# A two-layer streaming trunk on one core: the second chunk's loads queued behind the first's at the turn to the down products, and low parts and norm sums moved from POOL to DVE

## The chip, the cores and the metric

One core of a Trainium2 chip runs the whole program. The metric is the device time of one execution in microseconds (us). The engines are PE (TensorE: matmuls, with weight loads in PEld), DVE (VectorE), ACT (ScalarE), POOL (GpSimd) and SP (SyncE, which issues all the DMAs here). Each engine works through its own instructions in the order in which the program was written out; between engines, semaphores decide.

## The reference

Two layers on 1088 tokens (1024 of a prompt, 64 of running streams) with 1024 channels, in 32-bit floats. Layer 0 mixes tokens with a diagonal state-space model (S5) that ends in a gated linear unit, layer 1 with attention that has forget gates (FoX). Each is followed by a ConvFFN with 2816 hidden channels. Cut to what matters:

```python
def s5_mixer(...):            # layer 0
    ...
    val, gate = jnp.split(g @ w_glu, 2, axis=-1)
    return val * jax.nn.sigmoid(gate), ...

def fox_prompt(...):          # layer 1
    ...
    return o @ w_o, k, v, logf

def conv_ffn(x, hist, w_up, w_gate, conv_w, conv_b, w_down):
    a = x @ w_up
    ... # conv: three taps along the tokens
    h = jax.nn.gelu(conv + conv_b) * (x @ w_gate)
    return h @ w_down, a_pad[:, -(CONV_WIDTH - 1):]

for i in range(DEPTH):
    xp = xp + mixer(rms_norm(xp, norm_mix[i]))
    xp = xp + conv_ffn(rms_norm(xp, norm_ffn[i]), ...)
y = rms_norm(xp, norm_final)  # the same for xs, the 64 tokens of running streams
```

## The kernel before

**Numbers.** A 32-bit product is made of three matmuls on rounded parts: each operand is split into a high part (ACT copies it to a rounded type) and a low part (operand minus high part). hi x hi, hi x lo and lo x hi are added up in a PSUM bank. The 1088 tokens lie in four chunks of 272 columns, the channels on the 128 partitions. `k.x[d]` is the residual of channel block d, of 8.

**Plain weights.** `unit` (L116) loads a block of weights of 128 x 1024 (L121), makes hi on ACT (L125) and lo on POOL (L126). `kunit` calls it for the gated linear unit (GLU), for the query, key and value projections (qkv) and for the output projection (`wo`); `plain_unit` calls it for three pairs of hidden channel blocks of the down product. There are 85 such subtracts: 32 in GLU, 25 in qkv, 16 in wo, 6 in each FFN. The pools of raw, hi and lo have 2, 3 and 3 buffers.

**Seven products.** The other FFN weights go through Strassen's scheme: a product of 2 x 2 blocks is made of 7 block products instead of 8 (`SUMS`, j in the order 0, 1, 3, 2, 5, 4, 6). `left_factors` makes the 7 left factors of a weight block: POOL forms four sums (L312 to L315), ACT the high parts (L303) and DVE the low parts (L304). Its buffers of hi and lo are those of `unit`. `to_forms` makes the right factors of the normed input (L232, L233 the split, L239 the norm's scaling, L258 to L264 the sums), and `store_forms` those of a hidden pair (L473, L474, L481 to L487).

**The FFN.** A loop over the 11 hidden pairs fp makes up and gate products on PE (L335 in `block`); `channels` collects them, L554 multiplies the two, and `store_forms` writes the 7 forms of the pair to DRAM (544 KB each). The down products take the pairs in four chunks, `PCH` = (0, 1), (10, 2), (3, 4), (5, 6); pairs 7 to 9 are done plainly. `load(ci)` (L430) issues the loads of a chunk's forms: those of chunk 0 and 2 go to `k.R`, the buffers of the normed input's forms, which come free as the last gate products have read them; in the rows they are xh and xl. Those of chunk 1 and 3 go to `k.E` (e) or to a buffer b. The last pair, 10, stays in SBUF, so chunk 1 loads 7 forms only. `load(0)` is called in the last pass of the loop, and `load(ci + 1)` at the head of the down loop's pass ci. `reload` (L425) brings back residual blocks that were put aside in DRAM. The adds of down products into the residual are L585, on DVE; they free PE's PSUM banks. I call the place where PE goes from the last gate products to the down products the turn; the transpose of the conv tail (L564) stands between the two.

**Norm sums.** `Norm.add` squares a new residual block on ACT (L167) and adds it to a running sum (L168), on POOL for odd d and on DVE for even d. The GLU calls it after L1210 and L1212, the output projection after L1568.

**Order.** The order of instructions on each engine isn't the one of the text. A scheduler walks through the program with a model of the engines' times and writes out a fixed order for each engine; it may exchange instructions that do not depend on each other. All DMAs here are issued by SP, in eight lanes taken in turn: an issue waits until the transfer eight places before it has landed.

Of the kernel before, what the change touches and what calls it, by code (L numbers as in the profile page):

```python
# [9 lines left out]

F32 = mybir.dt.float32
F32R = mybir.dt.float32r
# [103 lines left out]
def unit(k, src, a, b, raw=None, to=None):  # L116

    nc = k.nc
    if raw is None:
        raw = k.wraw.tile([P, KT, 2 * P], F32, name="raw").rearrange("p a b -> p (a b)")[:, :a * b].rearrange("p (a b) -> p a b", b=b)  # L120
        nc.sync.dma_start(raw, src)  # L121
    if to is None:
        to = [q.tile([P, KT, P], F32R, name=m).rearrange("p a b -> p (a b)") for q, m in ((k.whi, "hi"), (k.wlo, "lo"))]
    hi, lo = (t[:, :a * b].rearrange("p (a b) -> p a b", b=b) for t in to)
    nc.scalar.activation(hi, raw, AF.Copy)  # L125
    nc.gpsimd.tensor_tensor(lo, raw, hi.bitcast(F32), op=OP.subtract)  # L126
    return hi, lo


# [274 lines left out]
def ffn(k, layer, norm, after, prepare=lambda: None):  # L404
# [11 lines left out]
    with ExitStack() as ctx:  # L416
# [10 lines left out]
                k.x[d] = xtile(k, d)[:, :T]  # L427
                nc.sync.dma_start(k.x[d], k.xD[d])

        def load(ci):  # L430

            for m, (j, _) in enumerate(SUMS):
                for n, fp in enumerate(PCH[ci]):
                    if (fp, j) in slots:
                        continue
                    if ci % 2 == 0:
                        t = k.R[2 + 2 * m + n]
                    elif 7 * n + m < 12:
                        t = k.E[7 * n + m]
                    else:  # L440
                        t = k.big.tile([P, T], F32R, name="b")
                    slots[fp, j] = t
                    nc.sync.dma_start(t.bitcast(F32), fD[fp][j])

        def load_plain(fps, tiles):
            for fp in fps:
# [100 lines left out]
        for fp in range(FP):  # L547
            cs, gs = channels(fp, None if fp else k.entry)
            if fp == FP - 1:
                unit0 = down_unit(0, 0)  # L550
                load(0)
            for c, g in zip(cs, gs):
                for o, w, s in parts(0, T):
                    v.tensor_tensor(g[:, o:o + w], c[:, o + 2 * s:o + 2 * s + w], g[:, o:o + w], op=OP.mult)  # L554
            turn = itertools.cycle((lambda: xtile(k, 2), lambda: xtile(k, 3), lambda: k.big.tile([P, T], F32, name="b")))
            if fp == FP - 1:
                reload((2, 3))
                store_forms(fp, gs)
            else:
                (store_plain if fp in PLAIN else store_forms)(fp, gs, lambda: next(turn)())  # L560
# [42 lines left out]

        for ci, fps in enumerate(PCH):
            if ci + 1 < len(PCH):
                load(ci + 1)
            else:
                load_plain(PLAIN[:1], iter(k.R[2:6]))
            for u in range(2):
                w = down_unit(ci, u) if ci or u else unit0  # L610
                for dd in range(2):
                    down(w, 2 * u + dd, dd * P, fps, (0, 1))
# [554 lines left out]
def glu(k, norm, after):  # L1167
# [13 lines left out]
    with tc.tile_pool(name="gl", bufs=1) as pool:  # L1181
        for a, hs in enumerate(HALVES):
            for d in range(KT):
                if d % 2 == 0:
                    raws = load((d * P, D + d * P), 1 if a or d else 2)
                wv, wg = (unit(k, None, KT, P, r[:, :, d % 2 * P:d % 2 * P + P]) for r in raws)
                if a == 0 and d == 4:
                    k.cw = [conv_params(k, pool, k.bank(), i) for i in range(2)]
                ps = {}

                def products(n, kts):
                    if n not in ps:
                        ps[n] = [k.bank() for i in range(2)]
                    for p, u in zip(ps[n], (wv, wg)):
                        dense(k, p, u, *NCH[n], kts)
                if a == 0 and d == 0:
                    for kts in (range(KT - 1), (KT - 1,)):
                        for n in hs:
                            products(n, kts)
                for n in hs:  # L1200
                    o, m = NCH[n]
                    if n not in ps:
                        products(n, range(KT))
                    if a == 0 and n == 0:
                        for i in (0, 1) if d == 0 else (d + 1,) if d + 1 < KT else ():
                            k.nc.sync.dma_start(k.x[i], k.x0D[i])
                    pv, pg = ps[n]
                    s = k.tmp.tile([P, CW], F32, name="tm")[:, :m]
                    nc.scalar.activation(s, pg[:, :m], AF.Sigmoid)
                    nc.vector.tensor_tensor(s, s, pv[:, :m], op=OP.mult)  # L1210
                    x = k.x[d][:, o:o + m]
                    nc.vector.tensor_tensor(x, x, s, op=OP.add)  # L1212
                    norm.add(n, d)
                if a and d < 2:
                    next(k.entry, None)
            k.entry = after(a)
# [341 lines left out]
def wo(k, norm, after):  # L1558
    nc, tc = k.nc, k.tc
    for a, hs in enumerate(HALVES):  # L1560
        for d in range(KT):
            u = kunit(k, k.I["fox_w_o"][0], d * P)
            for n in hs:
# [2 lines left out]
                dense(k, ps, u, o, m)  # L1566
                x = k.x[d][:, o:o + m]
                nc.vector.tensor_tensor(x, x, ps[:, :m], op=OP.add)  # L1568
                norm.add(n, d)
            if a and d < 2:  # L1570
                next(k.entry, None)
        k.entry = after(a)
# [119 lines left out]
```

## Time and profile before

| | us |
|---|---|
| median of 3 runs | 2690.65 |
| lowest, highest | 2681.59, 2690.93 |
| profiled execution | 2694.2 |
| its span | 2692.4 |

The stages of the span, roughly, in us:

| stage | from | to |
|---|---|---|
| state-space mixer | 0 | 290 |
| GLU | 290 | 505 |
| FFN 0, up and gate products | 497 | 977 |
| FFN 0, down products in four chunks | 977 | 1175 |
| FFN 0, plain down products | 1175 | 1240 |
| qkv (25 units) | 1240 | 1550 |
| attention | 1550 | 1835 |
| output projection | 1835 | 1937 |
| FFN 1, up and gate products | 1937 | 2421 |
| FFN 1, down products and final norm | 2421 | 2692 |

The profile shows one execution. An engine's busy share is an average over all stages; what a change in one stage is worth is read from that stage's rows. A number in brackets behind an instruction in the timeline is the time that its engine had waited for nothing else, and what released it. PEclk is the clock that TensorE was granted, as a share of full speed, 2.4 GHz.

### The profile page before, as it was taken

How to read it: one execution, taken by the hardware profiler on the slowest of the kernel's cores; microseconds unless marked ns; L12 is line 12 of the kernel's file. 1: busy time of each engine (PE TensorE's matmuls, PEld its weight loads, DVE VectorE, ACT ScalarE, POOL GpSimd, SP SyncE). 2: the span in 40 equal slices, each digit the busy share in tenths (PEclk: the TensorE clock that was granted, in tenths of full speed). 3: DMA queues.
4: the chain of work that ended last, by engine and by line, in shares of the span. 5: the costliest groups of instructions: out<-in, count | busy, mean ns of one | idle time of the engine just before them, and what ended most of it. 6: DMA issues, size and time to landing. Idle time of an engine off the chain costs nothing. (4 is left out here: it accounts for less than half of the span.)

```text
span 2692.4 us, 52353 instructions
## 1 busy us (share of the span) xinstructions
PE 2570.8 (95%) x20646; PEld 2418.3 (90%) x20646; DVE 1813.3 (67%) x3534; ACT 1127.4 (42%) x2190; POOL 1045.2 (39%) x938
## 2 busy tenths in 40 slices
PE   7788899999999999999999999999999999999998
PEld 4676899899999999999999966668999999999998
DVE  5899426878877668755322178883788877668865
ACT  5444324454444431124222277773454545441213
POOL 4576445533222222235212167774542222222222
PEclk9878999999999999999999999999999999999999
DMA  5112523234433377335686667753314433347531
GB/s 146 46 38 59 163 78 114 63 119 166 154 116 139 106 272 260 100 107 162 180 225 183 179 166 196 192 145 122 112 64 147 179 131 139 114 168 292 197 114 67
DMA packets 265739, 385.28 MB, mean 143 GB/s; under 512 B 27980, under 2 KB 210244, under 8 KB 265492
## 3 DMA queue, kind: packets, MB, share of 16 engines
q1 hardware_dynamic: 265492, 381.92, 45.1%
q8 instruction: 163, 2.67, 0.4%
q14 instruction: 84, 0.69, 0.1%
HBM read 251.31 MB, written 121.50 MB: 138 GB/s over the span
## 5 line engine op out<-in xcount | busy, mean ns | idle before, releaser
L335 PE MATMUL mm<-e,hi 128*128 128x272 f32 x2464 | 476.4, 290 | 7.2 <-ACT hi L303 7.2
L136 PE MATMUL mm<-xh,hi 128*128 128x272 f32 x1408 | 407.0, 290 | 1.6 <-DVE tm L1500 1.0
L138 PE MATMUL mm<-xh,lo 128*128 128x272 f32 x1408 | 404.7, 289 | 1.5 <-POOL lo L126 1.5
L335 PEld LDWEIGHTS mm<-e,hi 128*128 128x128 f32 x2464 | 387.6, 189 | 7.9 <-ACT hi L303 7.8
L137 PE MATMUL mm<-xl,hi 128*128 128x272 f32 x1280 | 368.8, 289 | 0.0
L335 PE MATMUL mm<-e,lo 128*128 128x272 f32 x1232 | 353.6, 289 | 2.4 <-DVE lo L304 2.4
L335 PE MATMUL mm<-xh,hi 128*128 128x272 f32 x1792 | 351.1, 291 | 2.7 <-DVE x L509 2.7
L303 ACT ACTIVATE hi<-raw 128x1024 fp32r<-128x1024 f32 x186 | 196.1, 1056 | 316.0 <-PE mm L335 254.3
L126 POOL TENSOR_TENSOR lo<-raw,hi 128x1024 fp32r<-128x1024 f32 (+1 forms) x83 | 198.6, 2398 | 327.9 <-ACT hi L125 303.7
L314 POOL TENSOR_TENSOR raw<-s,raw 128x512 f32<-128x512 f32 x62 | 91.0, 1468 | 581.3 <-DVE lo L304 580.0
L335 PE MATMUL mm<-xl,hi 128*128 128x272 f32 x1440 | 283.2, 291 | 15.5 <-DMA xl<-fD 9.5
L335 PEld LDWEIGHTS mm<-xh,hi 128*128 128x128 f32 x1792 | 284.5, 190 | 4.0 <-DVE x L509 3.5
L136 PEld LDWEIGHTS mm<-xh,hi 128*128 128x128 f32 x1408 | 265.6, 189 | 2.9 <-DVE tm L1500 1.5
L138 PEld LDWEIGHTS mm<-xh,lo 128*128 128x128 f32 x1408 | 264.7, 189 | 2.1 <-POOL lo L126 2.1
L304 DVE TENSOR_TENSOR lo<-raw,hi 128x1024 fp32r<-128x1024 f32 x186 | 245.3, 1319 | 22.9 <-ACT hi L303 22.8
L335 PE MATMUL mm<-xh,lo 128*128 128x272 f32 x896 | 258.8, 291 | 1.0 <-DVE lo L304 1.0
L585 DVE TENSOR_TENSOR x<-x,mm 128x272 f32<-128x272 f32 x512 | 201.9, 433 | 65.9 <-PE mm L335 63.9
L335 PEld LDWEIGHTS mm<-xl,hi 128*128 128x128 f32 x1440 | 229.0, 191 | 17.2 <-ACT e L473 9.9
L137 PEld LDWEIGHTS mm<-xl,hi 128*128 128x128 f32 x1280 | 241.6, 189 | 0.1
L335 PEld LDWEIGHTS mm<-e,lo 128*128 128x128 f32 x1232 | 232.2, 189 | 2.6 <-DVE lo L304 2.6
L335 PE MATMUL mm<-xl,lo 128*128 128x272 f32 x720 | 209.6, 292 | 0.0
L312 POOL TENSOR_TENSOR s<-raw 128x512 f32<-128x512 f32 x62 | 82.5, 1331 | 292.6 <-DVE s1l L304 274.6
(423 smaller groups left out, 6096.3 us busy)
## 6 DMA issues: line engine op xcount, KB each, us to landing
fD<-x SPq DMA_DIRECT2D x82, 544.0 KB
e<-fD SPq DMA_DIRECT2D x50, 544.0 KB
raw<-in_ffn_w_up SPq DMA_DIRECT2D x24, 1024.0 KB
raw<-in_ffn_w_gate SPq DMA_DIRECT2D x22, 1024.0 KB
fD<-b SPq DMA_DIRECT2D x40, 544.0 KB
xh<-fD SPq DMA_DIRECT2D x32, 544.0 KB
xl<-fD SPq DMA_DIRECT2D x32, 544.0 KB
raw<-in_ffn_w_down SPq DMA_DIRECT2D x64, 256.0 KB
```

Of the source, the lines that this page charges most:

```text
L126: nc.gpsimd.tensor_tensor(lo, raw, hi.bitcast(F32), op=OP.subtract)
L136: mm(ps, h, rh, start=first, stop=False)
L137: mm(ps, h, rl, start=False, stop=False)
L138: mm(ps, l, rh, start=False, stop=last)
L303: nc.scalar.activation(h, t, AF.Copy)
L304: nc.vector.tensor_tensor(l, t, h.bitcast(F32), op=OP.subtract)
L312: add(s1, a21, a22, op=OP.add)
L314: add(a11, s1, a11, op=OP.subtract)
L335: k.nc.tensor.matmul(bank[:, :CW], x, y, start=j not in (2, 4, 6) and n == 0 and i == 0, stop=n == last and i == 2, skip_group_check=True)
L585: v.tensor_tensor(x, x, bank[:, :m], op=OP.add)
```

## The change

Three edits:

- `load` links each load to the one before it with an order-only edge (`issue_after`): the scheduler has to keep the loads of a chunk in the order of the text and those of the next chunk behind them. `queued` carries the last load on to the next chunk.
- In `unit`, the low part (L126) is made by DVE instead of POOL.
- The norm sums of GLU and output projection (L168) are on DVE for every d; those of the other stages stay as they were.

```diff
@@ unit @@
     nc.scalar.activation(hi, raw, AF.Copy)
-    nc.gpsimd.tensor_tensor(lo, raw, hi.bitcast(F32), op=OP.subtract)
+    nc.vector.tensor_tensor(lo, raw, hi.bitcast(F32), op=OP.subtract)
     return hi, lo
@@ load @@
-        def load(ci):
+        def load(ci, ins=None):
...
                     slots[fp, j] = t
-                    nc.sync.dma_start(t.bitcast(F32), fD[fp][j])
+                    with tc.issue_after(ins) if ins else nullcontext():
+                        ins = nc.sync.dma_start(t.bitcast(F32), fD[fp][j]).ins
+            return ins
@@ ffn @@
                 unit0 = down_unit(0, 0)
-                load(0)
+                queued = load(0)
...
             if ci + 1 < len(PCH):
-                load(ci + 1)
+                queued = load(ci + 1, queued)
@@ glu @@
-                    norm.add(n, d)
+                    norm.add(n, d, k.nc.vector)
@@ wo @@
-                norm.add(n, d)
+                norm.add(n, d, nc.vector)
```

POOL's instructions go from 940 to 823 and DVE's from 3536 to 3653; PE's and SP's stay the same in number. The lines of the changed kernel are two higher behind `load`.

SP at the turn of layer 0, before: fD is the DRAM copy of the forms, and its second number the pair; xl_2018 and xl_2306 are the buffers of slot 4 of the seven sums, xl_2595 and xl_2820 of slot 5, xl_2946 and xl_2985 of slot 6.

```order
190 L443 DMA e_3057<-fD_2_5300 128x1088
191 L443 DMA xl_1730<-fD_1_5299 128x1088
192 L443 DMA xl_1442<-fD_0_5298 128x1088
193 L443 DMA e_3059<-fD_2_5300 128x1088
194 L443 DMA e_3058<-fD_2_5300 128x1088
195 L443 DMA b<-fD_2_5300 128x1088
196 L443 DMA xl_2306<-fD_1_5299 128x1088
197 L443 DMA xl_2018<-fD_0_5298 128x1088
198 L443 DMA e_3061<-fD_2_5300 128x1088
199 L443 DMA e_3060<-fD_2_5300 128x1088
200 L443 DMA xl_2820<-fD_1_5299 128x1088
201 L443 DMA xl_2595<-fD_0_5298 128x1088
```

The same place after:

```order
190 L444 DMA xl_1442<-fD_0_5298 128x1088
191 L444 DMA xl_1730<-fD_1_5299 128x1088
192 L444 DMA xl_2018<-fD_0_5298 128x1088
193 L444 DMA xl_2306<-fD_1_5299 128x1088
194 L444 DMA xl_2595<-fD_0_5298 128x1088
195 L444 DMA xl_2820<-fD_1_5299 128x1088
196 L428 DMA x_10797<-xD 128x1088
197 L444 DMA xl_2946<-fD_0_5298 128x1088
198 L444 DMA xl_2985<-fD_1_5299 128x1088
199 L444 DMA e_3057<-fD_2_5300 128x1088
```

All loads of pair 2 (e and b) have moved behind those of pairs 0 and 1, the pair of each slot has changed places, and a residual reload (x_10797) stands ahead of slot 6. The turn of layer 1 has the same pattern.

DVE at the same turn, before: L474 makes the low parts of the last pair's forms, L481 to L487 their sums, L585 adds down products to the residual.

```order
934 L474 TENSOR_TENSOR e_3051<-b,e_3051 128x544
935 L585 TENSOR_TENSOR x_3033<-x_3033,mm 128x272
936 L474 TENSOR_TENSOR e_3054<-b,e_3054 128x544
937 L481 TENSOR_TENSOR b<-b 128x544
938 L483 TENSOR_TENSOR b<-b 128x544
939 L474 TENSOR_TENSOR e_3052<-b,e_3052 128x544
940 L484 TENSOR_TENSOR b<-b 128x544
941 L474 TENSOR_TENSOR e_3055<-b,e_3055 128x544
942 L487 TENSOR_TENSOR b<-b 128x544
943 L474 TENSOR_TENSOR e_3053<-b,e_3053 128x544
944 L474 TENSOR_TENSOR e_3056<-b,e_3056 128x544
945 L585 TENSOR_TENSOR x_10552<-x_10552,mm 128x272 x2
```

After (L476 is the old L474, L483 and so on L481, L587 L585):

```order
975 L476 TENSOR_TENSOR e_3054<-b,e_3054 128x544
976 L587 TENSOR_TENSOR x_10554<-x_10554,mm 128x272 x2
977 L483 TENSOR_TENSOR b<-b 128x544
978 L587 TENSOR_TENSOR x_10552<-x_10552,mm 128x272 x2
979 L485 TENSOR_TENSOR b<-b 128x544
980 L587 TENSOR_TENSOR x_3034<-x_3034,mm 128x272
981 L476 TENSOR_TENSOR e_3052<-b,e_3052 128x544
982 L587 TENSOR_TENSOR x_3034<-x_3034,mm 128x272
983 L486 TENSOR_TENSOR b<-b 128x544
984 L587 TENSOR_TENSOR x_10552<-x_10552,mm 128x272
985 L587 TENSOR_TENSOR x_3033<-x_3033,mm 128x272
986 L587 TENSOR_TENSOR x_10552<-x_10552,mm 128x272
```

The adds that stood behind all pieces of the last pair now stand between them.

POOL at the end of the output projection, before: L312 to L315 are the sums of the first up weight's left factors in FFN 1.

```order
695 L126 TENSOR_TENSOR lo<-raw,hi 128x1024
696 L168 TENSOR_TENSOR s<-s,tm 128x272
697 L126 TENSOR_TENSOR lo<-raw,hi 128x1024
698 L233 TENSOR_TENSOR e_21682<-b,e_21681 128x544
699 L312 TENSOR_TENSOR s<-raw 128x512
700 L168 TENSOR_TENSOR s<-s,tm 128x272
701 L313 TENSOR_TENSOR raw<-raw 128x4x128
702 L168 TENSOR_TENSOR s<-s,tm 128x272
703 L314 TENSOR_TENSOR raw<-s,raw 128x4x128
704 L315 TENSOR_TENSOR raw<-raw 128x4x128
```

After:

```order
599 L233 TENSOR_TENSOR e_21676<-b,e_21675 128x544 x2
600 L233 TENSOR_TENSOR e_21682<-b,e_21681 128x544
601 L312 TENSOR_TENSOR s<-raw 128x512
602 L313 TENSOR_TENSOR raw<-raw 128x4x128
603 L233 TENSOR_TENSOR e_21682<-b,e_21681 128x544
604 L314 TENSOR_TENSOR raw<-s,raw 128x4x128
605 L315 TENSOR_TENSOR raw<-raw 128x4x128
```

The subtracts (L126) and norm sums (L168) are gone from POOL, and nothing but one split stands between its four weight sums. They stand on DVE, among the splits and sums of `to_forms`.

## Rows read from the trace of the kernel before

**Rows 1.** The page's part 1: busy time, share of the span and instructions.

```profile
PE 2570.8 (95%) x20646; PEld 2418.3 (90%) x20646; DVE 1813.3 (67%) x3534; ACT 1127.4 (42%) x2190; POOL 1045.2 (39%) x938
```

**Rows 2.** What PE waited for, 960 to 2693 us: total, times, longest.

```profile
PE mm L335 <- DMA xl<-fD: 9.5, 2, 5.1
```

**Rows 3.** Timeline of PE at both turns: start, length, instruction, wait before it.

```profile
981.60 0.40 PE L335 MATMUL mm<-xh,lo 128*128 128x272 f32 x1 [0.98 <-DVE lo L304]
...
988.81 0.79 PE L335 MATMUL mm<-xl,hi 128*128 128x272 f32 x2 [4.45 <-DMA xl<-fD]
...
2432.82 0.79 PE L335 MATMUL mm<-xl,hi 128*128 128x272 f32 x2 [5.08 <-DMA xl<-fD]
```

**Rows 4.** Timeline of SP's DMA issues at the turn of layer 0.

```profile
973.15 1.02 SPq L443 DMA_DIRECT2D e<-fD  x2
975.15 0.32 SPq L443 DMA_DIRECT2D b<-fD  x1
976.55 1.68 SPq L443 DMA_DIRECT2D xl<-fD  x2
979.26 1.68 SPq L443 DMA_DIRECT2D e<-fD  x2
```

**Rows 5.** Stretches of both turns: busy by engine, then clock, DMA share, GB/s.

```profile
core 0: us, PE busy (x) PEld busy (x) DVE busy (x) ACT busy (x) POOL busy (x), PEclk, DMA share, GB/s
976.00:988.00 12.00, 7.38 (x57) 6.93 (x56) 11.93 (x21) 3.69 (x7) 1.51 (x1) 1.00 1.03 411
988.00:996.00 8.00, 7.19 (x36) 7.22 (x37) 5.87 (x11) 1.91 (x3) 0.00 (x0) 0.57 0.92 357
996.00:1010.00 14.00, 14.00 (x115) 14.00 (x114) 11.06 (x24) 3.82 (x4) 5.21 (x4) 1.00 0.56 191
...
2420.00:2432.00 12.00, 7.74 (x61) 7.33 (x59) 11.93 (x22) 4.29 (x7) 0.00 (x0) 0.99 1.03 408
2432.00:2440.00 8.00, 7.18 (x36) 7.21 (x37) 5.34 (x10) 1.32 (x2) 0.00 (x0) 0.58 1.03 408
2440.00:2454.00 14.00, 14.00 (x114) 14.00 (x113) 11.65 (x24) 3.70 (x4) 4.31 (x4) 1.00 0.58 202
```

**Rows 6.** Groups by line and shape: count, busy us, mean ns, idle before.

```profile
L126 POOL TENSOR_TENSOR lo<-raw,hi 128x1024 fp32r<-128x1024 f32 x80 | 193.5, 2423 | 313.7 <-ACT hi L125 289.5 <-DMA raw<-in_ssm_w_glu 17.1 <-PE y L1126 5.6
L168 POOL TENSOR_TENSOR s<-s,tm 128x272 f32<-128x272 f32 x62 | 52.9, 853 | 90.1 <-ACT tm L167 88.4 <-DMA raw<-in_ssm_w_glu 1.7
L304 DVE TENSOR_TENSOR lo<-raw,hi 128x1024 fp32r<-128x1024 f32 x186 | 245.3, 1319 | 22.9 <-ACT hi L303 22.8
L585 DVE TENSOR_TENSOR x<-x,mm 128x272 f32<-128x272 f32 x512 | 201.9, 433 | 65.9 <-PE mm L335 63.9
L1313 DVE TENSOR_TENSOR ql<-pe,qh 128x272 fp32r<-128x272 f32 x32 | 22.7, 730 | 48.3 <-DMA kD<-ql 31.3 <-ACT qh L1312 17.0
```

**Rows 7.** Who waited for L126 (us, times), over the whole span.

```profile
PE mm L138: 1.5, 2
```

**Rows 8.** Stretches at the end of the output projection, columns as in rows 5.

```profile
1896.00:1928.00 32.00, 32.00 (x255) 31.77 (x254) 31.39 (x45) 14.59 (x25) 20.21 (x12) 1.00 0.46 151
1928.00:1940.00 12.00, 8.62 (x69) 8.40 (x68) 8.47 (x10) 4.87 (x9) 10.21 (x7) 1.00 0.01 2
1940.00:1948.00 8.00, 6.75 (x34) 6.72 (x34) 4.83 (x11) 3.35 (x7) 4.80 (x4) 0.57 0.42 132
```

**Rows 9.** There: timelines of POOL, DVE and PE, and the chain of waits between.

```profile
1920.53 2.74 POOL L126 TENSOR_TENSOR lo<-raw,hi 128x1024 fp32r<-128x1024 f32 x1 [2.36 <-ACT hi L125]
...
1921.28 2.58 DVE L264 TENSOR_TENSOR b<-b 128x544 f32<-128x544 f32 x1
...
1928.07 0.77 POOL s L168
...
1930.10 1.13 POOL s L168
1931.23 0.54 issue
...
1941.25 0.82 PE L335 MATMUL mm<-e,hi 128*128 128x272 f32 x2 [4.63 <-ACT hi L303]
```

More of the change, by code (lines that the diff above doesn't have):

```diff
@@ L8 @@
 import math
-from contextlib import ExitStack, contextmanager
+from contextlib import ExitStack, contextmanager, nullcontext
 F32 = mybir.dt.float32
```

## The prediction

> **What bounds the kernel now.** I read the engine totals first. PE is busy for 2570.8 of 2692.4 us, DVE for 1813.3 and POOL for 1045.2 [rows 1], so a change pays only where PE waits, or where a wait drops PE's clock afterwards. The second view is the list of what PE waited for behind the first gate products: the largest entry is the loads of stored forms, 9.5 us in two waits [rows 2]. The timeline of PE has both, at the turn from the gate products to the down products of each layer: 4.45 us before 988.81 and 5.08 us before 2432.82 [rows 3]. Ahead of the first stands a wait of 0.98 us for a low part from DVE. The third view, stretches of each turn, tells what else is lost: behind the wait the granted clock is 0.57 and 0.58 of full speed for 8 us, which is mostly the lower level, 1.2 GHz, and 1.00 in the stretch after it, 2.4 GHz [rows 5]. PE does 36 matmuls in 7.19 us there and 115 in 14.00 us later; at the later rate the 36 would take 36 x 14.00 / 115 = 4.4 us, so the clock costs 2.8 us a turn. The DMA share is 1.03 with some 410 GB/s through the wait, so the load is late because the transfers run back to back and the needed one stands far back among them.
>
> The same reading at the end of the output projection gives a second place: PE waits 4.63 us for a high part (ACT L303) before 1941.25 [rows 9], and the next 8 us have a clock of 0.57 [rows 8].
>
> **Part 1, the loads.** Before, SP issues two chunk-2 forms (e) at 973.15 and one more (b) behind them, then xl_2306 and xl_2018 from 976.55 on and two more e's at 979.26 [rows 4]. With e_3057, which stands ahead of the first xl pair, five transfers that precede xl_2018 will follow it: e, e, e, b and xl_2306, whose place is exchanged with it (the order of SP above). One pair is issued 2.71 us after another (976.55, 979.26), 1.36 us for a form of 544 KB; 0.557 MB at 411 GB/s [rows 5] is 1.36 us too. PE goes on with xl_2018 at 988.81 when it has landed; five transfers less is 6.8 us earlier, 982.0. PE wants it at 984.36, where its wait begins (988.81 - 4.45). xl_2306 follows 1.4 us behind, at 983.4, and is used later than xl_2018. So the DMA wait should vanish, with 2.4 us to spare. The released slots allow it: the gate products that last read these slots end in the last 6 us ahead of the tail's transpose, at about 971 to 977. The second chunk is wanted some 50 us later (four chunks fill the 198 us of the down stage in the table above), and its 7 forms are 10 us of transfers, so pushing it back costs nothing while that distance holds; without it each form would cost 1.36 us. The order-only link itself adds no instruction and no semaphore, as it ties neighbours on one queue.
>
> What is late next is DVE. In the first turn's 34 us it is busy 11.93 + 5.87 + 11.06 = 28.86 us, in the second 11.93 + 5.34 + 11.65 = 28.92 [rows 5]. It forms the last gate channel, the low parts of the down weights and the adds that empty PE's banks; PE consumes what it makes within a few microseconds. If all this has to be done by the time PE has done its matmuls, the stretch can shrink by DVE's idle time alone, 5.1 us in each turn. Without DVE's bound it would shrink by 4.45 + 2.8 = 7.25 and 5.08 + (7.18 - 36 x 14.00 / 114) = 7.8 us. DVE's order after puts the adds between the pieces of the last channel, which helps PE get banks. I take DVE's bound, **-10.2 us** for both turns; the ends are -15.1 us and 0.
>
> One thing goes against it: the reload of x_10797, which waits for a product of DVE's gate work, now stands ahead of xl_2946 and xl_2985 on SP. They hold slot 6, the last of the seven sums: PE's new order has 56 matmuls between xl_2018 and xl_2946, 56 x 14.00 / 115 = 6.8 us, and five transfers between the two take 6.8 us as well, so the 2.4 us to spare hold there too. I put it at 0; a reload that is held for more than 2.4 us would go straight to PE.
>
> **Part 2, subtracts and sums from POOL to DVE.** POOL loses 85 subtracts of 2.42 us and 32 sums of 0.85 us, 233 us [rows 6]. DVE gets 85 x 1.32 (its own subtracts of the same shape, L304) and 32 x 0.43 (an add of the same shape, L585) = 126 us, and would be busy for 1939 of 2692 us. Nearly all of it lies beside PE: PE waited for a POOL subtract only 1.5 us in all [rows 7]. In GLU that wait goes: **-1 us**, ends -1.5 and +2 (four sums of 0.43 us, should they stand on the way to the norm). In the qkv stage a subtract now queues behind DVE operations that wait for stores, 31.3 us of idle in 32 instances of L1313 [rows 6]. The 25 units fill 310 us (the table above), so one lasts PE some 12 us, and a low part has three buffers, so the nearest row says 0. The plain units of the FFN have six subtracts a layer, 8 us of DVE in stretches where PE waits for nothing: 0, and the whole 8 us if that cover were gone.
>
> At the output projection the sum is close. DVE is busy for 31.39 of 32 us between 1896 and 1928 [rows 8], so work added there can come out at the end. Four subtracts and four sums are 4 x 1.32 + 4 x 0.43 = 7.0 us. But DVE is slowed there by POOL: L264 at 1921.28 takes 2.58 us beside POOL's subtract at 1920.53 [rows 9], while the 272-column add takes 0.43, so 544 columns should take some 0.8: 1.8 us come back from each such meeting. I count four meetings, 7 us, and put the two against each other: 0. What is left is POOL's chain, which ended last here: two norm sums of 0.77 and 1.13 us and 0.54 us of issue stand between POOL's sums of the first up weight [rows 9] and are gone, 2.4 us. With them goes part of the clock's loss (34 matmuls in 6.75 us against 255 in 32.00, up to 2.5 us): I take **-4 us**. The ends are -7.1 (4.63 + 2.5: the whole wait and the clock) and +4.6 (7.0 - 2.4: no meeting relieved).
>
> A rule of the notes bears on this and against the change: the Trainium skill, "SBUF — State Buffer", section "Who interferes with whom", says that a DVE instruction with two SBUF inputs contends with a GpSimd instruction that reads SBUF, each holding the shared ports for its whole length. The 2.58 us of L264 agrees. The moved subtract also has two SBUF inputs, so by that rule it meets POOL's weight sums instead; L304's 1.32 us, a mean over instances beside such sums, has this in it.
>
> **Sum.** -10.2 - 4 - 1 = -15.2 us. Against the profiled execution, 2694.2 us (span 2692.4 and 1.8 around it), that is 2679.0. The median of the runs is 2690.65, 0.13% below the profiled execution; in this proportion the forecast is **2675.5 us**, -0.56%. About 0.5% (13.5 us: under 2677.2 or over 2704.1) is what a measurement of this kernel can tell from no change.
>
> **Rivals.**
> *DVE is worse than a bound at the turn.* It works 11.93 of 12 us before the wait [rows 5], and PE already waits 0.98 us there for a low part [rows 3]. If the adds and the last channel's pieces are still in PE's way, half of 5.1 us is gained a turn: -5.1 - 4 - 1 = -10, 2680.6. For it: DVE has no slack in just these microseconds. Against it: its new order interleaves the adds.
> *The new queue order does not land earlier.* SP's issue is held by full queues and by the release of the slots, and x_10797 holds the queue from its new place. Then both turns give 0, and -5 remains: 2685.6. Against it: DMA is saturated already from before the transpose, so taking bytes out of the front must show.
> *DVE is overloaded (the other side).* Where DVE is full, at the end of the output projection, the 7.0 us come out in full; each subtract meets a POOL sum and costs 2.4 instead of 1.32 us (+4.3), and the longer wait keeps the clock low for another stretch (+2.8): +14 there. At the end of GLU, with the same shape of work, the same again: +28 - 10.2 = +18, 2708. It turns slower than before from the point at which the added DVE work that reaches PE exceeds the 10 us from the turns. Against it: POOL's 233 us are gone, and with them most meetings.
>
> **How the numbers follow.** Forecast 0.50, DVE at the turn 0.24, no earlier landing 0.14, overload 0.12. The forecast's own ends are -15.1 - 7.1 - 1.5 = -23.7 (2667) and about 2684. The range reaches to the rivals of small gain and holds part of the overload, and 4 us more below, as one run of before was 9 us under the others: 2663 to 2692. Faster by over 0.5%: 0.48 (most of the forecast with what lies beyond it, little of the others); within 0.5%: 0.42; slower by over 0.5%: 0.10.
>
> **What would show it.** Right: at the turns PE has no wait for xl over 1 us, the clock stays near 1.00 in the 8 us behind, DVE is busy for nearly all of the turn, the e loads stand behind xl_2985; no POOL row of L126; the wait at the end of the output projection is under 3 us. Wrong: a wait of the same size at the turn under another name (low part, x reload), or PE waiting for DVE's L239, L233 or L304 longer than now at the ends of GLU and of the output projection.

## The result, and the profile after

| | before | after |
|---|---|---|
| median, us (6 runs each) | 2690.79 | 2664.68 |
| lowest, highest | 2681.15, 2696.16 | 2663.84, 2674.54 |
| ratio, 95% interval | | 0.9923 [0.9902, 0.9945] |
| span of the profiled execution | 2692.4 | 2662.3 |

The change makes the kernel 0.8% faster. The forecast, 2675.5 us, was 11 us too high, and the time lies near the lower end of the range. One further execution of before, of 4049 us at a granted clock of 0.558, was in a slow state and is left out of every comparison. Of the 30 us between the two profiled executions, 13 lie in the state-space mixer, in which the change orders nothing differently; the sections below come back to them. Here is the page of after, engines first:

```profile
span 2662.3 us, 52270 instructions
...
PE 2570.1 (97%) x20646; PEld 2418.4 (91%) x20646; DVE 1849.0 (69%) x3651; ACT 1128.6 (42%) x2190; POOL 831.2 (31%) x821
```

PE does the same work as in [rows 1] in a span that is 30 us shorter. POOL has lost 214 us, and DVE has gained only 36, not the 126 of the forecast. Some 18 us of that gap are not the change's: the trace of before holds one very long DVE product (e8 to e10 below), and e1, which has DVE's instructions of before without it, has DVE busy for 1795.2 us. Against that the gain is 54. The rest of the gap is that DVE's own operations are shorter beside a POOL that works less. The groups by line and shape of after (count, busy us, mean ns) show it; in [rows 6] POOL's subtract took 2423 ns and DVE's own 1319:

```profile
L126 DVE TENSOR_TENSOR lo<-raw,hi 128x1024 fp32r<-128x1024 f32 x80 | 98.5, 1239 | 80.6 <-ACT hi L125 70.7 <-DMA raw<-in_ssm_w_glu 5.9 <-PE y L1128 3.8
L168 DVE TENSOR_TENSOR s<-s,tm 128x272 f32<-128x272 f32 x82 | 45.0, 549 | 24.9 <-ACT tm L167 23.0 <-ACT nt L186 1.3 <-POOL s L168 0.6
L1214 DVE TENSOR_TENSOR x<-x,tm 128x272 f32<-128x272 f32 x32 | 14.9, 469 | 0.8
```

L1214 is the old L1212, which took 930 ns before (868 in e1, where nothing was moved):

```profile
L1212 DVE TENSOR_TENSOR x<-x,tm 128x272 f32<-128x272 f32 x32 | 29.7, 930 | 0.9
```

The turn of layer 0, in stretches of the same lengths from the transpose on as in [rows 5] (columns as there):

```profile
962.20:974.20 12.00, 12.00 (x98) 12.00 (x98) 12.00 (x25) 3.81 (x7) 0.00 (x0) 1.00 1.03 410
974.20:982.20 8.00, 8.00 (x66) 8.00 (x66) 8.00 (x17) 3.38 (x5) 1.50 (x1) 1.00 0.96 332
982.20:996.20 14.00, 14.00 (x114) 14.00 (x114) 13.21 (x31) 2.12 (x2) 5.01 (x4) 1.00 0.85 293
```

PE is busy without a gap, the clock stays at 1.00 (2.4 GHz), and DVE is full for 20 us and nearly full for 14 more. SP's issues at that turn, to be held against [rows 4]:

```profile
954.38 6.72 SPq L444 DMA_DIRECT2D xl<-fD  x6
962.62 0.32 SPq L428 DMA_DIRECT2D x<-xD  x1
963.34 1.33 SPq L444 DMA_DIRECT2D xl<-fD  x2
965.70 0.32 SPq L444 DMA_DIRECT2D e<-fD  x1
```

All six loads of slots 3 to 5 are issued by 961.10, before the transpose at 963.1, and the reload of x waits 1.5 us at most and holds nothing up. What PE waited for in the FFN's matmuls at the end of the output projection and the start of FFN 1 (1800 to 1976 us of after: total, times, longest):

```profile
PE mm L335 <- ACT hi L303: 3.6, 2, 2.6
PE mm L335 <- DVE lo L304: 2.4, 1, 2.4
PE mm L335 <- DVE x L511: 1.2, 1, 1.2
```

The wait of 4.63 us in [rows 9] has become 2.55:

```profile
1919.74 0.52 PE L335 MATMUL mm<-e,hi 128*128 128x272 f32 x2 [2.55 <-ACT hi L303]
```

To see where the time went I cut each trace at the same instructions: the first matmul of GLU (L136), the conv tail's transpose at either turn (L564), the first and the last add of the plain down products (L602), the first transpose of qkv (L1250), the first scores (L1473), the first add of the output projection (L1568). Two of these cuts, before and then after, as the traces list them (first and last start):

```profile
L564 PE MATMUL mm<-ident,tail x2: 271/272/273, 976.8 to 2421.2; 128*88 128x128 f32 x2
L602 DVE TENSOR_TENSOR x<-x,mm x128: 423/439/441, 1154.7 to 2680.0; 128x272 f32<-128x272 f32 x128
```

```profile
L566 PE MATMUL mm<-ident,tail x2: 271/272/272, 963.1 to 2397.4; 128*88 128x128 f32 x2
L604 DVE TENSOR_TENSOR x<-x,mm x128: 422/436/440, 1132.6 to 2648.6; 128x272 f32<-128x272 f32 x128
```

So 976.8 to 1154.7 is 177.9 us before, and 963.1 to 1132.6 is 169.5 after. The whole table, with the kernels of the next section, in us:

| kernel | mixer | GLU to turn 0 | turn 0 to plain | plain to qkv | qkv and attention | output proj. to turn 1 | turn 1 to last add | end |
|---|---|---|---|---|---|---|---|---|
| before | 290.1 | 686.7 | 177.9 | 104.3 | 578.8 | 583.4 | 258.8 | 12.4 |
| after | 277.1 | 686.0 | 169.5 | 106.3 | 579.4 | 579.1 | 251.2 | 13.7 |
| loads alone (e1) | 277.9 | 686.8 | 169.2 | 104.3 | 579.2 | 584.6 | 251.1 | 12.8 |
| moves alone (e2) | 276.4 | 685.7 | 176.2 | 106.4 | 579.2 | 581.1 | 257.7 | 12.3 |
| low parts alone (e3) | 289.5 | 683.4 | 175.2 | 106.3 | 579.3 | 581.6 | 257.5 | 12.4 |
| norm sums alone (e4) | 280.4 | 687.0 | 176.0 | 104.3 | 579.3 | 580.5 | 257.2 | 13.2 |
| after, again (e5) | 279.6 | 685.3 | 169.5 | 104.8 | 580.1 | 577.7 | 251.2 | 13.1 |
| plain low parts on POOL (e6) | 280.6 | 683.6 | 169.3 | 105.0 | 580.1 | 580.2 | 251.2 | 13.0 |
| DVE work added (e7) | 288.9 | 686.6 | 173.7 | 104.8 | 579.5 | 580.0 | 256.0 | 13.5 |
| after, WC on DVE (e8) | 269.0 | 685.0 | 169.5 | 104.8 | 579.4 | 580.3 | 251.5 | 13.7 |
| before, WC on DVE (e9) | 276.2 | 684.4 | 176.1 | 104.3 | 578.0 | 583.6 | 258.2 | 12.4 |
| as e8 (e10) | 273.7 | 682.7 | 169.4 | 106.4 | 579.0 | 579.9 | 251.4 | 12.9 |

### The profile page after: what moved, and what is told of

Read it like the earlier page. It is cut to its first block, busy times and chain, and to the rows that moved or that the text cites. A ratio compares the mean times of both kernels' runs of the same rounds, so it can differ in the third digit from the quotient of the medians.

```text
span 2662.3 us, 52270 instructions
## 1 busy us (share of the span) xinstructions
PE 2570.1 (97%) x20646; PEld 2418.4 (91%) x20646; DVE 1849.0 (69%) x3651; ACT 1128.6 (42%) x2190; POOL 831.2 (31%) x821
## 5 line engine op out<-in xcount | busy, mean ns | idle before, releaser
L335 PE MATMUL mm<-e,hi 128*128 128x272 f32 x2464 | 475.5, 289 | 4.4 <-ACT hi L303 4.4
L136 PE MATMUL mm<-xh,hi 128*128 128x272 f32 x1408 | 407.5, 290 | 2.9 <-ACT hi L125 1.4
L335 PEld LDWEIGHTS mm<-e,hi 128*128 128x128 f32 x2464 | 386.9, 189 | 5.0 <-ACT hi L303 4.9
L335 PE MATMUL mm<-e,lo 128*128 128x272 f32 x1232 | 353.2, 289 | 2.4 <-DVE lo L304 2.4
L335 PE MATMUL mm<-xh,hi 128*128 128x272 f32 x1792 | 349.3, 289 | 3.6 <-DVE x L511 3.5
L335 PEld LDWEIGHTS mm<-xh,hi 128*128 128x128 f32 x1792 | 282.5, 189 | 5.0 <-DVE x L511 4.7
L335 PE MATMUL mm<-xl,hi 128*128 128x272 f32 x1440 | 279.8, 289 | 4.8 <-ACT hi L303 3.2
L136 PEld LDWEIGHTS mm<-xh,hi 128*128 128x128 f32 x1408 | 266.0, 189 | 4.0 <-ACT hi L125 1.6
L335 PE MATMUL mm<-xh,lo 128*128 128x272 f32 x896 | 257.5, 289 | 0.0
L587 DVE TENSOR_TENSOR x<-x,mm 128x272 f32<-128x272 f32 x512 | 200.2, 430 | 53.6 <-PE mm L335 51.6
L335 PEld LDWEIGHTS mm<-e,lo 128*128 128x128 f32 x1232 | 231.9, 189 | 2.6 <-DVE lo L304 2.6
L335 PEld LDWEIGHTS mm<-xl,hi 128*128 128x128 f32 x1440 | 226.1, 188 | 6.4 <-ACT hi L303 3.6
L335 PE MATMUL mm<-xl,lo 128*128 128x272 f32 x720 | 207.9, 289 | 0.0
L312 POOL TENSOR_TENSOR s<-raw 128x512 f32<-128x512 f32 x62 | 84.8, 1369 | 316.4 <-DVE s1l L304 268.9
L374 ACT ACTIVATE tm<-mm 128x272 f32<-128x272 f32 x264 | 101.4, 388 | 162.7 <-PE mm L335 157.9
## 6 DMA issues: line engine op xcount, KB each, us to landing
raw<-in_ffn_w_down SPq DMA_DIRECT2D x64, 256.0 KB
```

Of the source, the lines that this page charges most:

```text
L136: mm(ps, h, rh, start=first, stop=False)
L312: add(s1, a21, a22, op=OP.add)
L335: k.nc.tensor.matmul(bank[:, :CW], x, y, start=j not in (2, 4, 6) and n == 0 and i == 0, stop=n == last and i == 2, skip_group_check=True)
L374: nc.scalar.activation(t, bank[:, :CW], AF.Copy)
L587: v.tensor_tensor(x, x, bank[:, :m], op=OP.add)
```

## The experiments

My theory was that each part works in its own place: the loads at the turns, the moved work at the end of the output projection. The rivals were that the turn needs the moved work too, since DVE is full there, and that the moved work costs elsewhere what it gives. The first four ran on one chip, with before at 2682.12 us (31 runs).

**e1, the loads alone.** The change without its other two edits:

```diff
-                    nc.sync.dma_start(t.bitcast(F32), fD[fp][j])
+                    with tc.issue_after(ins) if ins else nullcontext():
+                        ins = nc.sync.dma_start(t.bitcast(F32), fD[fp][j]).ins
```

> Edit: the load chain alone; low parts and norm sums stay on POOL. Theory (each part works in its own place): both turns lose their wait for xl, 178 us from the tail's transpose to the first plain add becomes about 170 and the same at layer 1, so 16 us less than before in the trace from the GLU on; the wait at the end of the output projection stays at 4.6 us. Rival (the turn's gain needs the moved work too, since DVE's order and load decide it): the wait for xl goes, but a wait for DVE of 3 to 5 us a turn takes its place, 6 to 10 us less. Besides: a stall of some 10 us near 75 us of the span, in the state-space mixer, may be there or not, in any of the kernels, since nothing is changed there.

Measured: 2671.78 us, ratio 0.9959 [0.9940, 0.9977]. Both turns shrink as in after (169.2 and 251.1 us), and in its trace PE has no wait in L335 between 955 and 1010 us. At the output projection the wait is the old one, in the timeline of PE:

```profile
1920.82 0.82 PE L335 MATMUL mm<-e,hi 128*128 128x272 f32 x2 [4.62 <-ACT hi L303]
```

The turn's gain comes from the loads alone; the rival falls. From the GLU on the trace is 14.3 us shorter than before, where 16 were expected, and the medians differ by 10.3 us.

**e2, the moves alone.** Low parts and norm sums on DVE, `load` as before:

```diff
-    nc.gpsimd.tensor_tensor(lo, raw, hi.bitcast(F32), op=OP.subtract)
+    nc.vector.tensor_tensor(lo, raw, hi.bitcast(F32), op=OP.subtract)
...
-                norm.add(n, d)
+                norm.add(n, d, nc.vector)
```

> Edit: low parts and norm sums on DVE, loads as before. Theory: the turns keep their waits of 4 to 5 us for xl and the half clock behind them; the wait at the end of the output projection shrinks from 4.6 to 2.6 us as in the changed kernel; 3 to 5 us less than before from the GLU on, in all. Rival (the moved work is what freed the turn): the turns shrink by 3 us or more each without the loads' order. Rival (moved work only hides behind the gain at the turns): slower than before from the GLU on by 2 us or more.

Measured: 2678.15 us, ratio 0.9982 [0.9962, 1.0002]: not to be told from before by the times. By the trace it is 3.7 us shorter than before from the GLU on (2675.0 - 276.4 against 2692.4 - 290.1), but unchanged code scatters by as much: e9 below, which differs from before only ahead of the GLU, is 5.3 us shorter there (2397.0). So what the moves give in all can't be read from this pair of traces; the table is better read by stretch. PE's wait for xl stays at the turns (4.1 us each); that at the end of the output projection falls to 2.54. "Plain to qkv" is 2.1 us longer.

**e3 and e4, one move each.** e3 has the first of the two edits of e2, e4 the second, in GLU and in the output projection.

> Edit: the low parts alone on DVE; norm sums on POOL, loads as before. If the gain at the end of the output projection comes from the sums that stood in POOL's chain, the wait for the high part stays at 4 us or more there and the time is that of before within 2 us from the GLU on. If it comes from DVE being rid of POOL's subtracts, the wait falls to 2.6 us and 2 to 4 us are gained.

> Edit: the norm sums alone on DVE; low parts on POOL, loads as before. If the sums in POOL's chain are the cause at the end of the output projection, the wait falls to about 2.6 us and 3 to 4 us are gained from the GLU on; if the subtracts are, it stays at 4 us or more.

Measured: e3 2679.06 us, 0.9994 [0.9972, 1.0016]; e4 2679.65 us, 0.9989 [0.9969, 1.0009]. Neither differs from before in the times. The wait at the end of the output projection is 2.46 us in e3 and 3.24 us in e4. Timeline of PE in e3, then in e4:

```profile
1934.96 0.53 PE L335 MATMUL mm<-e,hi 128*128 128x272 f32 x2 [2.46 <-ACT hi L303]
```

```profile
1929.10 0.52 PE L335 MATMUL mm<-e,hi 128*128 128x272 f32 x2 [3.24 <-ACT hi L303]
```

Against before that is 2.2 and 1.4 us less, and both moves together do no more than the low parts alone. But e9, in which nothing was moved, has a wait of 3.70 us there, so the sums' share of the wait may be as little as 0.5. By the whole stretch from the output projection to turn 1 the sums do no worse: 580.5 us in e4, 581.6 in e3, 583.4 to 584.6 with neither move (before, e1, e9). Either move seems to help, and their shares were not separated. My prediction had named the sums alone.

**e5 and e6, the plain down products.** On another chip (before 2683.73 us, 20 runs). The traces of after, e2 and e3 had 106 us in "plain to qkv", those with POOL's low parts 104.3, and PE waited 1.5 us for L190 there, in front of which DVE had a low part. e5 is the changed kernel once more; e6 has the six plain low parts of each layer on POOL again:

```diff
-    nc.vector.tensor_tensor(lo, raw, hi.bitcast(F32), op=OP.subtract)
+    (eng or nc.vector).tensor_tensor(lo, raw, hi.bitcast(F32), op=OP.subtract)
...
-            return unit(k, src[:, :, nd * u * P:nd * (u + 1) * P], nf, nd * P, to=to)
+            return unit(k, src[:, :, nd * u * P:nd * (u + 1) * P], nf, nd * P, to=to, eng=nc.gpsimd)
```

> The changed kernel itself, on the same chip as the three below. Theory: from the GLU on it is 17 us shorter than before in the trace; its times fall into two groups some 10 us apart, as those of before do (2678 to 2685 and 2688 to 2694 on one chip), by whether one DVE operation near 70 us of the span (the product Q of the state-space mixer) takes 2 or over 10 us; against the lower group of before it is 15 us faster.

> Edit: the changed kernel, with the six low parts of the plain down products of each layer back on POOL. Theory (one of these subtracts stands ahead of the norm's last step on DVE): the stretch from the first plain add to the first transpose of qkv goes from 106.3 to 104.3 us, and PE's wait of 1.5 us for nr goes; 2 to 3 us faster than the changed kernel. Rival (the 2 us there come from another place): 106 us as before.

Measured: e5 2662.9 us, 0.9921 [0.9894, 0.9948]; e6 2672.85 us, 0.9944 [0.9924, 0.9964]. From the GLU on e5 is 20.6 us shorter than before in the trace, and the mean of its four lower runs is 18.6 under the lower group of before on this chip (17 and 15 were expected). Six of e6's ten runs lie in the upper of two groups of times that e8 to e10 are about, against one of e5's five, so their medians are not to be compared. In e6 the wait is still there, in the list of what PE waited for between 1120 and 1242 us:

```profile
PE mm L200 <- DVE nr L190: 1.5, 1, 1.5
```

and the stretch takes 105.0 us against 104.8 in e5. The theory falls: the plain low parts aren't the cause. But they are not the ones that stand ahead of L190 either. POOL has made all six by 1160.2 us of e6, and DVE still has a low part right in front of L190:

```profile
1204.77 1.23 DVE L126 TENSOR_TENSOR lo<-raw,hi 128x1024 fp32r<-128x1024 f32 x1 [0.26 <-ACT hi L125]
1205.91 0.72 DVE L190 SCALAR_TENSOR_TENSOR nr<-nt,nr 128x3 f32<-128x3 f32 x1
```

It belongs to a unit of qkv, which e6 leaves on DVE; whether that one makes PE wait was not tried. Why the same wait costs 0.5 us in e5 and 2 in after can be read: it is 1.49 us long in both, and in the stretch of 8 us behind it the granted clock is 0.79 in after and 1.00 in e5, with 53 matmuls against 64 (first after, then e5):

```profile
1206.00:1214.00 8.00, 8.00 (x53) 7.85 (x52) 7.26 (x16) 4.12 (x10) 4.04 (x5) 0.79 0.80 293
```

```profile
1208.00:1216.00 8.00, 8.00 (x64) 7.89 (x63) 7.49 (x17) 5.00 (x13) 5.19 (x6) 1.00 0.85 306
```

**e7, more DVE work at the turn.** The seven low parts of the last pair's forms are made twice:

```diff
-                v.tensor_tensor(q[:, H:], t, q[:, :H].bitcast(F32), op=OP.subtract)
+                for _ in range(2 if stage is None else 1):
+                    v.tensor_tensor(q[:, H:], t, q[:, :H].bitcast(F32), op=OP.subtract)
```

> Edit: the changed kernel, in which the seven low parts of the last pair's forms are made twice on DVE (the same values written again), 7 x 0.71 = 5 us more of DVE work at each turn. Theory A (DVE is what bounds the turn, as the prediction has it): each turn gets 4 to 5 us longer, 174 instead of 169.5 us from the transpose to the first plain add. Theory B (much of DVE's work at the turn can wait): under 1.5 us a turn.

Measured: 2683.79 us, 0.9993 [0.9976, 1.0010], by the median no gain over before. But half of that is not the turns' doing: eight of the ten runs lie in the upper group of times, against seven of before's twenty, and the profiled execution has the longer mixer. Group against group e7 is 7 to 8 us under before, and 10 to 11 over e5. The turns take 173.7 and 256.0 us, 4.2 and 4.8 more than in e5, for 5.0 us of added work. The third stretch of its first turn, on the columns of [rows 5], and what PE waited for there:

```profile
994.60:1008.60 14.00, 11.30 (x79) 9.99 (x79) 14.00 (x26) 3.77 (x5) 3.98 (x3) 1.00 0.42 148
```

```profile
PE mm L335 <- DVE lo L304: 2.1, 2, 1.5
PE mm L335 <- DVE x L588: 0.5, 1, 0.5
```

DVE is full in this stretch and in the two before it, 34 us in all, and PE waits for it. Theory A: behind the change DVE is the next bound of the turn, with less than 1 us to spare.

**e8, e9 and e10, the long product in the mixer.** The traces of before, e3 and e7 have a mixer of 289 to 290 us, the others of the same mixer code one of 276 to 281, with the same order of instructions on every engine. The cause is one DVE operation. Before, timelines of DVE, POOL (its first and last three rows) and PE:

```profile
70.46 13.59 DVE L1003 TENSOR_TENSOR Q<-P,Bst 128x512 f32<-128x512 f32 x2 [1.85 <-PE s L1008]
```

```profile
70.31 2.28 POOL L990 TENSOR_TENSOR WC<-P,Cd 128x576 f32<-128x576 f32 x2
72.56 0.61 POOL L710 TENSOR_TENSOR g<-EE,UU 128x256 f32<-128x256 f32 x1
73.14 0.61 POOL L711 TENSOR_TENSOR g<-EE,UU 128x256 f32<-128x256 f32 x1
...
81.17 0.61 POOL L710 TENSOR_TENSOR g<-EE,UU 128x256 f32<-128x256 f32 x1
81.75 0.61 POOL L711 TENSOR_TENSOR g<-EE,UU 128x256 f32<-128x256 f32 x1
82.44 1.06 POOL L712 TENSOR_TENSOR E<-g,g 128x256 f32<-128x256 f32 x1
```

```profile
82.97 0.69 PE L1008 MATMUL s<-sel,Q 128*128 128x64 f32 x2 [10.38 <-DVE Q L1003]
```

The first of two products Q takes 12.46 us (the longest of 32, whose median is 990 ns). It starts 0.15 us behind the first of the two products WC, in a row of POOL operations without a gap, and ends at 82.92, 0.56 us behind that row's first pause (82.36 to 82.44); PE waits 10.38 us for it. After, the same two products:

```profile
72.65 1.95 DVE L1005 TENSOR_TENSOR Q<-P,Bst 128x512 f32<-128x512 f32 x2 [4.33 <-PE s L1010]
```

```profile
72.84 0.61 POOL L713 TENSOR_TENSOR g<-EE,UU 128x256 f32<-128x256 f32 x1
74.90 1.17 POOL L992 TENSOR_TENSOR wt<-P,Cd 128x576 f32<-128x576 f32 x1 [1.46 <-ACT Cd L983]
```

They start 2.2 us later and fall on a place at which POOL waits for 1.46 us. So the times of before lie in two groups, 2677 to 2686 and 2688 to 2697 (37 of 92 runs in the upper), and those of the changed kernel too (2 of 11 in the upper); whether the change alters how often the upper group comes isn't settled by so few. e8 and e10 are the changed kernel, e9 the one before, each with the first block's part of that row on DVE:

```diff
-    OPT = [0, 1, 0, 0, 0, 0]
+    OPT = [0, 1, 0, 0, 1, 0]
```

> Edit: the changed kernel, with the six products and sums of the first block's WC in the state-space mixer on DVE instead of POOL (an option that the code has), which takes 7 us out of POOL's unbroken row of operations there. Theory (POOL's unbroken row holds up the DVE product that runs beside it): no Q over 3 us, one group of times alone, none 8 us or more above the lowest; the mixer takes 277 us or up to 4 us more for DVE's added work. Rival (the long product comes from elsewhere): runs 10 us above the lowest remain.

> Edit: the kernel before, with the six products and sums of the first block's WC on DVE, as in the run on the changed kernel. Theory (the long product Q does not come from the change and the change does not act on it): its times fall into one group, 22 to 26 us under the upper group of before, and the mixer takes about 269 us; against the next kernel it is 15 to 17 us slower, which is then the change's effect without that disturbance. Rival (the change has a part in the mixer's time): the distance to the next kernel is over 20 us.

> Edit: the changed kernel with the same six operations on DVE, on the same chip. Theory: 2655 to 2659 us, one group of times, 0.6% under the kernel above and about 1% under before.

Measured: e8 2657.84 us, 0.9895 [0.9869, 0.9921]; e9 2675.04 us, 0.9964 [0.9950, 0.9979]; e10 2660.65 us, 0.9910 [0.9889, 0.9932]. In all three traces no Q is over 2.0 us. e8 and e10 span 2654.9 to 2662.1 us in 10 runs; e9 spans 2669.2 to 2681.0 in 12, wider than I said, but with no gap of over 3.4 us in it. It misses in another point: it lies 16.5 us under the upper group of before (2691.5 in the mean, same chip), not 22 to 26, and its mixer takes 276.2 us, not 269. e8's mixer takes 269.0, where 277 to 281 were expected, and e10 lies 1.7 us above the end of its range. e9 is 6.4 us under the lower group of before as well (2681.5), so moving the row to DVE gives something without the long Q too, which was not followed up. e10 is 14.4 us under e9, and that is what the change gives when the long Q plays no part (15 to 17 were expected). It also stands in the times of the changed kernel itself: against the two lower runs of before (2681.15 and 2681.59) the five lower ones of after (2663.84 to 2665.28) are some 17 us shorter, and e5 gave 18.6. The other 9 us of the measured 26 are the upper group, in which four of before's six runs lie and one of after's.

By the medians e8 is the fastest of all: 2657.84 us against 2662.9 for the changed kernel (e5, same chip). Their intervals against before overlap.

**e11 and e12, a longer row on POOL.** The changed kernel; the two products wt of the first block are made three times:

```diff
-                    we.tensor_tensor(o, p[:, gh, :, None].to_broadcast(sh), c[:, hs, None, :].to_broadcast(sh), op=OP.mult)
+                    for _ in range(3 if b == 0 and o is wt else 1):
+                        we.tensor_tensor(o, p[:, gh, :, None].to_broadcast(sh), c[:, hs, None, :].to_broadcast(sh), op=OP.mult)
```

> Edit: the changed kernel, in which POOL makes each of the two products wt of the first block three times (the same values again), 4 x 1.15 = 4.6 us more in POOL's unbroken row beside Q. Theory (Q is held until POOL's row has a gap): in a run of the upper group Q takes 14 to 18 us, and the upper group stands 12 to 15 us above the lowest times instead of 10. Rival (its length has nothing to do with POOL's row): 12.5 us and 10 us as before.

> The same kernel as e11_pool_more (wt of the first block made three times on POOL), again, since the profile there fell on an execution without the long Q. Theory: if the profiled execution is of the upper group, its Q takes 14 to 18 us and POOL has no gap beside it; the upper group of times stands 12 to 15 us above the lower one. Rival: 12.5 us and 10 us.

Measured: 2667.52 us, 0.9948 [0.9927, 0.9970], and 2667.2 us, 0.9928 [0.9906, 0.9950]. In neither was the profiled execution one of the upper group, so the long Q itself was not seen. In the times the upper group (four and two runs) stands 13.2 and 13.6 us above the lower one, mean against mean. In before, beside e11 and e12, the groups are 10.1 and 11.4 us apart. The row was 4.6 us longer, the step is 2 to 3 us longer, within the 12 to 15 us that the theory named, with few runs in each group: it goes the way of the theory, and the size was not settled.

## Why the prediction held, step by step

**The turns: right in mechanism, too small in size.** The wait for xl is gone at both turns, the clock stays up, and e1 ties both to the loads alone. The term was -10.2 us. Between the profiled executions it is -8.4 and -7.6, 16.0 in all, just over the end of -15.1; as a mean over the traces with either order of loads (five with the old: 176.3 and 257.9 us; those with the new except e7: 169.4 and 251.2) it is -6.9 and -6.7, 13.6 in all. The sum of wait and clock without DVE's bound, 7.25 and 7.8, which I had kept as an end of the range, is nearer than the bound that I took. The step that failed is the bound: I took all the work that DVE does in 34 us of before as work that PE must have by then. The groups by line of those 34 us, before and then after, show what it is made of:

```profile
L585 DVE TENSOR_TENSOR x<-x,mm 128x272 f32<-128x272 f32 x33 | 12.8, 432 | 3.0 <-PE mm L335 2.9
L474 DVE TENSOR_TENSOR e<-b,e 128x544 fp32r<-128x544 f32 x7 | 5.0, 719 | 0.1
```

```profile
L587 DVE TENSOR_TENSOR x<-x,mm 128x272 f32<-128x272 f32 x49 | 18.8, 427 | 0.8 <-PE mm L335 0.6
L476 DVE TENSOR_TENSOR e<-b,e 128x544 fp32r<-128x544 f32 x7 | 5.1, 723 | 0.0
```

The pieces of the last pair (L474) are wanted only in the second chunk, and the adds may lag behind PE as long as banks are free. What binds, then, is the first moment at which PE finds no bank or no low part, not the sum over the stretch. This is argued from the program and these rows; no run separates work that may wait from work that may not. That DVE is close to the bound was right all the same: e7 gives 5.0 us more to DVE, on the very pieces that are wanted later, and each turn gets 4.2 and 4.8 us longer, as DVE keeps its fixed order. The reload of x ahead of slot 6 cost nothing, as put down.

**The output projection: right in size, in part right in cause.** -4 was forecast; the stretch to turn 1 is 583.4 against 579.1, -4.3. The wait fell from 4.63 to 2.55 us, half of the gain; behind it the granted clock is 0.79 for 8 us (1918.5 to 1926.5 of after), where it was 0.57 in [rows 8]. How much of the rest is the clock's was not separated. But the cause wasn't the sums in POOL's chain alone, while low parts and DVE's relief cancel: e3 moves the low parts alone and has the shorter wait.

**GLU: not to be told.** -1 was forecast, and the stretch takes 686.7 against 686.0 us; but it scatters from 682.7 to 687.0 over the traces, so the table can't show a term of this size.

**qkv: right.** 0 forecast, 291.3 us before and 291.7 after between the first transpose and the first scores.

**Plain down products: a small loss that was not forecast.** 0 forecast with 8 as the bound; +2.0 in the pair of traces, +0.5 on the chip of e5. PE's wait of 1.5 us for L190 is in both, and the clock behind it makes the difference. e6 shows that the subtracts I had in mind aren't its cause; one of qkv's stands there, for which I had put 0, and it was not tried alone.

**DVE's load: wrong.** I expected 1939 us of DVE in all, and it is 1849. I let four meetings with POOL at the output projection be relieved, and left all the others out; and the base of 1813 had the long Q in it.

**The sum.** -15.2 was forecast; from the GLU on the traces give 2402.3 - 2385.2 = 17.1 us, and e10 against e9 14.4 us in the medians. The measured median moved by 26, and it was luck that the range still held it: its lower end had been widened because one run of before was 9 us under the others, and that run was the lower group. From that group (2681.4) the forecast's -15.2 gives 2666.2 us; the five lower runs of after have 2664.6 in the mean. The rest is the long Q, which I had not read: it stands in the trace of before as a wait of PE of 10.4 us, in a stage that the change doesn't touch, and I took that trace's time as the base without asking which runs have it.

The rivals: a worse DVE at the turn and no earlier landing are ruled out by after's turn and by e1; the overload at the output projection by the shorter wait and the shorter stretch.

## What to carry to other kernels

When a load is late in a saturated queue, count the transfers ahead of it that nobody wants yet; moving them back by an order-only edge costs no instruction, and the gain is the wait plus what the dropped clock cost behind it. The idle time of the next engine bounds such a gain only for work that the bound engine must have at once; sort its work by when it is wanted before taking the sum (argued here from one miss, not tried). And read the waits of the stages that the change leaves alone, too: one that is there in some executions only shifts the median by more than the change.

## What the runs showed of the hardware

A DVE operation with two inputs in SBUF can be held up by POOL far longer than one POOL operation lasts: Q, 990 ns in the median, took 12.46 us while POOL went through 14 operations of 0.6 to 1.4 us each without a gap (before, e3 and e7). With the first block's part of that row on DVE the long Q is gone (e8 to e10). The Trainium skill, "SBUF — State Buffer", section "Who interferes with whom", says that a DVE instruction with two SBUF inputs contends with a GpSimd instruction that reads SBUF, that the shared ports are an exclusive lock, and, of DVE's 2-port modes, that whoever issues first has them for the whole instruction while the other blocks. Here the wait did not end with the instruction that had them first. A row without a gap is not enough for it: two products Q at 66.89 us of before lie in the same row and took 1.72 us together. Why DVE did not get its turn between two of POOL's, as it does in most places (the longest L168 before is 2.4 us beside a POOL subtract of 2.4), was not settled.

Whether it happens goes with TensorE's clock. Stretches around it, in e3 with the long Q and then in after without:

```profile
60.00:70.00 10.00, 8.53 (x57) 7.21 (x55) 2.31 (x5) 7.79 (x24) 3.76 (x8) 1.00 0.71 238
70.00:84.00 14.00, 3.60 (x26) 2.87 (x27) 13.60 (x2) 1.99 (x5) 12.98 (x15) 0.71 0.08 21
```

```profile
60.00:70.00 10.00, 8.54 (x40) 7.05 (x40) 2.31 (x5) 7.46 (x21) 3.60 (x7) 0.67 0.71 239
70.00:84.00 14.00, 13.79 (x94) 12.29 (x94) 5.58 (x7) 7.29 (x16) 12.54 (x15) 0.74 0.18 46
```

The granted clock between 60 and 70 us was 0.85, 1.00 and 1.00 in before, e3 and e7, and 0.67 to 0.81 in the eight traces without the long Q that have this row on POOL (e11 and e12 with their longer row among them). With the higher clock PE released Q after 1.85 us of waiting instead of 3.3 to 4.3, straight behind the start of the first product WC. So the faster PE goes with a mixer that is some 10 us longer. The clock alone does not do it: e8 has 1.00 there, its row is on DVE, and no Q of it is long. That the clock is the cause where the row is on POOL was not tried; the traces only go together.
